# The S5 scan's output products for two state tiles at a time

## The chip, the cores and the metric

The kernel runs on one NeuronCore of a Trainium2 chip. A core has TensorE (matrix products, results in PSUM), VectorE, ScalarE, GpSimd and SyncE, which work side by side, each through its own queue in order, and DMA engines that move data between HBM and the on-chip memory SBUF. The metric is the time of one execution in microseconds on the device. The profiles show each instruction of one execution; the granted TensorE clock is given as a share of full speed.

## The reference

Two layers of an encoder for 256 tokens of width 1024, in float32. Layer 0 normalizes, projects, and splits its columns between an RWKV-7 recurrence (8 heads of 64) and an S5 diagonal state space model; both are concatenated and projected, then come cross-attention to a memory of 256 tokens and a dense SwiGLU. Layer 1 has differential attention, the same cross-attention, and eight SwiGLU experts, two for each token. What matters here is the S5 part: 32 groups of 16 channels, 64 complex states in a group.

```python
_, states = lax.associative_scan(combine, (jnp.broadcast_to(lam_bar, bu.shape), bu), axis=1)
c_mat = lax.complex(c_re.astype(F32), c_im.astype(F32))
y = jnp.real(jnp.einsum('gip,btgp->btgi', c_mat, states))
y = y + d_skip.astype(F32).reshape(S5_GROUPS, S5_GROUP) * ug
y = jax.nn.gelu(y.reshape(b, t, S5_WIDTH))
return y * jax.nn.sigmoid(y @ w_glu.astype(F32) + b_glu.astype(F32))
```

## The kernel before

The program is written in a tile framework. The code issues instructions on named engines; a planner then puts them in an order for each engine, by their priority (mostly the order in which the code issues them) and by a simulated timeline of when each input is ready, and it hands out buffer slots and adds the waits. A pool gives each tag a fixed number of slots; a tile that finds no slot waits until an older tile of its tag is released by its last reader.

The work runs in stages. From about 130 to 350 us three things are mixed, interleaved by `pipeline` (lines 1017 to 1044): the RWKV block matrices and states (`block_matrices`, `block_states`, `block_output`), the S5 scan as a side chain (`s5_scan`), and as filler the key and value projections of both memory attentions (`memory_kv`: cast `fwh` on ScalarE at L450, remainder `fwl` on VectorE at L453, products `pf` at L190 to L192), then the S5 gate (`s5_gate`) and the first half of the output projection. Then come the attention, the dense SwiGLU, layer 1 and the experts, all of which read weights from HBM.

The S5 scan handles the 2048 states in 16 state tiles of 128 rows. Tile j belongs to channel block m = j // 4 and to quarter q = j % 4 of it. For each tile:

- `inputs(j)`: two products of 32 rows into PSUM (`pbu`), VectorE multiplies them with a table into `xc` (L561) and `zz` (L562), GpSimd adds and subtracts (L563, L564);
- `scan(j)`: two scans over 256 tokens on VectorE (L569), `zz` from `xc`; the rotation back: `xc` on VectorE (L571), `zz` on VectorE or GpSimd by turns (L574), and two additions on GpSimd into `xc` (L575, L576), which are the last readers of `zz`;
- `outputs(j)`: two products, `cpad` by the real and by the imaginary half of `xc`, summed into rows 32q to 32q+31 of the PSUM tile `py`, so into a 32-column strip of TensorE's array. Each is shown as two matmul records, since the operands are full float32.

The loop runs `outputs(j - 2)`, `inputs(j)` and `scan(j - 1)` in step j. When the four tiles of a block are in `py`, `gelu(m)` reads it: VectorE L591, ScalarE L593 (the first write of the temporary `t1`), VectorE L594, ScalarE L595, VectorE L596. After steps 5 and 9 the tables of blocks 2 and 3 are made (`s5_table`). `xc`, `zz` and `t1` come from the pool `s5w` with two slots for each tag; `s5_gate` uses `t1` too (L956).

Of the kernel before, what the change touches and what calls it, by code (L numbers as in the profile page):

```python
# [8 lines left out]
F32 = mybir.dt.float32  # L9
# [8 lines left out]
T = 256  # L18
# [53 lines left out]
S5N = 0  # L72
# [51 lines left out]
def kernel(ctx: ExitStack, tc: tile.TileContext, a: dict, out: bass.AP, dbg=None):  # L124
# [10 lines left out]
    def scoped(cx, name, bufs, **kw):  # L135
        return cx.enter_context(tc.tile_pool(name=name, bufs=bufs, reuse_waits="tile", **kw))
# [15 lines left out]
    def col(name, i=0):  # L152
        lo, hi = COLS[name]
        return cols[:, lo + i:lo + i + 1]
# [33 lines left out]
    def mm3(out, lt, r, start, stop, **kw):  # L188

        nc.tensor.matmul(out, lhsT=lt[0], rhs=r[0], start=start, stop=False, **kw)  # L190
        nc.tensor.matmul(out, lhsT=lt[0], rhs=r[1], start=False, stop=False, **kw)  # L191
        nc.tensor.matmul(out, lhsT=lt[1], rhs=r[0], start=False, stop=stop, **kw)  # L192

    def mm(out, lt, r, start=True, stop=True, **kw):
        nc.tensor.matmul(out, lhsT=lt, rhs=r, start=start, stop=stop, **kw)  # L195
# [35 lines left out]
    cx = ExitStack()  # L231
    s5t = scoped(cx, "s5t", 2)
    s5w = scoped(cx, "s5w", 2)
    s5 = scoped(cx, "s5", 1)
    hk = scoped(cx, "hk", 1)
    rk = scoped(cx, "rk", 1)
# [84 lines left out]
    cpad = s5.tile([128, 2, 16, 32], F32, name="cpad")  # L321
# [79 lines left out]
    def s5_table(m):  # L401

        iota = C("iota")
        tbl = s5t.tile([128, 4, 2, T], F32, name="tbl", tag="tbl")
        for q in range(4):
            jc = lambda v: v[:, 4 * m + q:4 * m + q + 1]
            c, s = tbl[:, q, 0], tbl[:, q, 1]
            if TA[m] == "a":
                nc.scalar.activation(s, iota, AF.Copy, bias=MAGIC, scale=jc(fr))
            else:  # L410
                nc.vector.tensor_scalar(s, iota, jc(fr), MAGIC, op0=ALU.mult, op1=ALU.add)
            nc.scalar.activation(c, iota, AF.Copy, scale=jc(fh))
            gstt(c, s, MAGIC, c, op0=ALU.subtract, op1=ALU.subtract)
            gstt(s, iota, jc(fl), c, op0=ALU.mult, op1=ALU.subtract)
        c, s = tbl[:, :, 0], tbl[:, :, 1]
        gts(s, s, 0.5, -0.5, op0=ALU.min, op1=ALU.max)
        nc.scalar.activation(c, s, AF.Abs)
        nc.scalar.activation(c, c, AF.Sin, scale=-6.283185, bias=halfpi)
        nc.scalar.activation(s, s, AF.Sin, scale=6.283185)
        tables.append(tbl)  # L420
# [125 lines left out]
    def s5_scan():  # L546


        xs, zs, pys = {}, {}, {}
        bc2 = lambda v: v[:, None, :].to_broadcast([128, 2, T])  # L550

        def inputs(j):
            m, q = j // 4, j % 4
            rows = slice(32 * q, 32 * q + 32)
            sc = tables[m][:, q]
            pbu = ps_tr.tile([128, 2, T], F32, name="pbu", tag="tr")
            for ri in range(2):
                mm(pbu[:, ri], sbw[rows, ri, m], uT[rows, m])
            xc = xs[j] = s5w.tile([128, 2, T], F32, name="xc", tag="xc")
            z = zs[j] = s5w.tile([128, 2, T], F32, name="zz", tag="zz")  # L560
            nc.vector.tensor_tensor(xc, pbu, bc2(sc[:, 0]), op=ALU.mult)  # L561
            nc.vector.tensor_tensor(z, pbu, bc2(sc[:, 1]), op=ALU.mult)  # L562
            gtt(xc[:, 0], xc[:, 0], z[:, 1], op=ALU.add)  # L563
            gtt(xc[:, 1], xc[:, 1], z[:, 0], op=ALU.subtract)  # L564

        def scan(j):
            xc, z, sc = xs[j], zs[j], tables[j // 4][:, j % 4]
            for ri in range(2):
                nc.vector.tensor_tensor_scan(z[:, ri], rho[:, j:j + 1].to_broadcast([128, T]), xc[:, ri], 0.0,  # L569
                                             op0=ALU.mult, op1=ALU.add)  # L570
            nc.vector.tensor_tensor(xc, z, bc2(sc[:, 0]), op=ALU.mult)  # L571
            e_ = nc.gpsimd if SG[j] == "g" else nc.vector
            if not S5N:
                e_.tensor_tensor(z, z, bc2(sc[:, 1]), op=ALU.mult)  # L574
                gtt(xc[:, 0], xc[:, 0], z[:, 1], op=ALU.subtract)  # L575
                gtt(xc[:, 1], xc[:, 1], z[:, 0], op=ALU.add)  # L576
                return
            e_.tensor_tensor(z[:, 0], z[:, 0], sc[:, 1], op=ALU.mult)
            e_.scalar_tensor_tensor(z[:, 1], z[:, 1], -1.0, sc[:, 1], op0=ALU.mult, op1=ALU.mult)

        def outputs(j):
            m, q = j // 4, j % 4
            if q == 0:
                pys[m] = ps_po.tile([128, T], F32, name="py", tag="po")
            terms = ((0, xs[j][:, 0]), (1, xs[j][:, 1]), (1, zs[j][:, 0]), (0, zs[j][:, 1]))[:4 if S5N else 2]
            for i, (c, x) in enumerate(terms):
                mm(pys[m][32 * q:32 * q + 32], cpad[:, c, j], x, i == 0, i == len(terms) - 1)

        def gelu(m):

            nc.vector.scalar_tensor_tensor(yb[:, m], uT[:, m], col("s5_d", m), pys[m], op0=ALU.mult, op1=ALU.add)  # L591
            t1 = s5w.tile([128, T], F32, name="t1", tag="t1")
            nc.scalar.activation(t1, yb[:, m], AF.Square, scale=math.sqrt(0.044715))  # L593
            nc.vector.scalar_tensor_tensor(t1, t1, 1.0, yb[:, m], op0=ALU.add, op1=ALU.mult)  # L594
            nc.scalar.activation(t1, t1, AF.Tanh, scale=GELU_C)  # L595
            nc.vector.scalar_tensor_tensor(yb[:, m], t1, 1.0, yb[:, m], op0=ALU.add, op1=ALU.mult)  # L596

        for j in range(18):
            if j > 1:
                outputs(j - 2)  # L600
            if j < 16:
                inputs(j)
            if 0 < j < 17:
                scan(j - 1)
            yield 1.3, S5_LAT
            if j > 4 and j % 4 == 1:
                gelu((j - 2) // 4)
            if j in (5, 9):
                s5_table(2 + j // 8)
# [81 lines left out]
    for br, dst in ((0, lw), (1, av)):  # L691
        s = slice(br * 64, br * 64 + 64)
        for m2 in range(2):
            p = ps_mm.tile([128, 2, T], F32, name="pm", tag="mm")
            for j in range(2):
                m = 2 * m2 + j
                mm(p[:, j], wlr[s, m * 128:(m + 1) * 128], zr[s, 0])
            for j in range(2):
                m = 2 * m2 + j
# [244 lines left out]
    def s5_gate():  # L944
        gh, gl = ymix_h[:, 4:8], ymix_l[:, 4:8]
        nc.scalar.activation(gh, yb, AF.Copy, scale=0.5)
        nc.vector.scalar_tensor_tensor(gl, yb, 0.5, gh, op0=ALU.mult, op1=ALU.subtract)
        p = [ps_tr.tile([128, 2, T], F32, name="pm", tag="tr") for _ in range(2)]
        for k, wh, wl in chunks(a["w_glu"], 4):
            for m in range(4):  # L950
                ms = slice(m * 128, m * 128 + 128)
                mm3(p[m // 2][:, m % 2], (wh[:, ms], wl[:, ms]), (gh[:, k], gl[:, k]),
                    k == 0 and m % 2 == 0, k == 3, skip_group_check=True)
            yield 1.3
        for m in range(4):
            t1 = s5w.tile([128, T], F32, name="t1", tag="t1")  # L956
            nc.scalar.activation(t1, p[m // 2][:, m % 2], AF.Tanh, scale=0.5, bias=hcol[:, 8 + m:9 + m])
            nc.vector.scalar_tensor_tensor(yb[:, m], t1, 1.0, yb[:, m], op0=ALU.add, op1=ALU.mult)
        nc.vector.tensor_scalar(yb, yb, 0.25, None, op0=ALU.mult)
        if "yb" in dbg:  # L960
            for m in range(4):
                nc.sync.dma_start(dbg["yb"].rearrange("t (m c) -> m c t", c=128)[m], yb[:, m])
        nc.scalar.activation(ymix_h[:, 4:8], yb, AF.Copy)
        nc.vector.tensor_tensor(ymix_l[:, 4:8], yb, ymix_h[:, 4:8], op=ALU.subtract)
# [26 lines left out]
    def filler():  # L991
        yield from memory_steps
        for _ in s5:
            pass
        yield from s5_gate()
        yield from hy_first()

    s5 = s5_scan()

    def chain():  # L1000
# [1207 lines left out]
```

## Time and profile before

| | |
|---|---|
| three runs | 1668.07, 1673.05 and 1673.32 us, median 1673.05 |
| the profiled execution | 1672.61 us, its span 1670.8 us |
| TensorE busy | 1619.4 us, 97% of the span, 14882 matmul records |
| VectorE, ScalarE, GpSimd busy | 639.9, 476.1, 198.5 us |
| mean granted TensorE clock | 0.976 |
| output products `py` | 64 records, from 132.0 to 266.4 us |

Busy time is the time in which at least one instruction of an engine ran. Matmul records overlap in TensorE's pipeline, so a busy TensorE is not one at its peak; how long a matmul really holds the engine is read from the start of one to the start of the next. The chain of waits follows the work that ended last back from the end: at each step to what released it.

### The profile page before, as it was taken

The page shows a single profiled execution, that of the slowest core. Times are in us where ns is not written, and L with a number is a line of the kernel's source. Part 1 is how long each engine was busy: PE and PEld are TensorE (multiplying, and loading weights), DVE is VectorE, ACT ScalarE, POOL GpSimd, SP SyncE. Part 2 cuts the span into 40 slices and gives each one's busy share as a digit, 9 for nine tenths or more (in the row PEclk, how much of TensorE's full clock was granted, in tenths as well). Part 3 has the DMA queues.
Part 4 walks back from the last instruction along what each step waited for, and adds up shares of the span by engine and source line. Part 5 has one row for each costly group of instructions (what it writes and reads, how often), then busy time and mean ns, then how long its engine had stood idle before and what let it go on. Part 6 is the DMA issues. An engine that isn't in the chain of part 4 may idle for free.

```text
span 1670.8 us, 34308 instructions
## 1 busy us (share of the span) xinstructions
PE 1619.4 (97%) x14882; PEld 982.9 (59%) x14882; DVE 639.9 (38%) x1065; ACT 476.1 (28%) x852; POOL 198.5 (12%) x230
## 2 busy tenths in 40 slices
PE   6999999999999999999999999999999999999997
PEld 5877657899999988998334333343333433333432
DVE  7778987676555567764100011100101001010011
ACT  6466434555544456653101000010000100010000
POOL 6334473111000031110000000000000000000000
PEclk9999979999999999998999999999999999999999
DMA  6423323664555543646699889999999999999995
GB/s 227 152 89 127 109 71 115 222 255 152 186 193 180 195 156 116 239 150 239 252 387 383 333 356 407 415 418 419 419 418 418 419 419 419 418 419 387 372 419 218
DMA packets 74462, 471.48 MB, mean 282 GB/s; under 512 B 8600, under 2 KB 10008, under 8 KB 22464
## 3 DMA queue, kind: packets, MB, share of 16 engines
q1 hardware_dynamic: 73024, 465.02, 71.5%
q0 software_dynamic: 1280, 4.20, 0.7%
q8 instruction: 118, 1.93, 0.5%
q14 instruction: 40, 0.33, 0.1%
HBM read 463.94 MB, written 5.24 MB: 281 GB/s over the span
## 4 chain that ended last, share of the span: by engine, by line
PE 86%; DVE 8%; ACT 2%; POOL 2%; issue 2%; DMA 0%; SPq 0%; DVEq 0%; POOLq 0%; ACTq 0%
PE pgu L195 31%; PE pd L195 16%; PE pm L190 5%; PE pm L192 5%; PE pm L191 5%; PE pgu L190 2%; PE pgu L192 2%; PE pgu L191 2%; PE pm L195 2%; PE pgt L195 1%; PE pf L190 1%; PE pf L191 1%; PE pf L192 1%; PE po L195 1%; DVE zz L569 1%
## 5 line engine op out<-in xcount | busy, mean ns | idle before, releaser
L195 PE MATMUL pgu<-raw,gx 128*32 128x512 f32 (+1 forms) x5376 | 515.8, 542 | 0.0
L195 PEld LDWEIGHTS pgu<-raw,gx 128*32 128x32 f32 x5376 | 171.9, 110 | 319.8 <-issue 287.2
L195 PE MATMUL pd<-raw,th 128*32 128x512 f32 x2352 | 266.4, 607 | 0.4 <-DVE th L1896 0.4
L184 DVE TENSOR_TENSOR wl<-raw,wh 128x1024 fp32r<-128x1024 f32 (+1 forms) x159 | 195.0, 1238 | 103.2 <-ACT wh L178 102.8
L178 ACT ACTIVATE wh<-raw 128x1024 fp32r<-128x1024 f32 (+1 forms) x160 | 165.5, 1047 | 146.8 <-PE pgu L191 67.7
L1882 DVE SCALAR_TENSOR_TENSOR actA<-pgu,gs,actA 128x512 f32<-128x512 f32 (+1 forms) x32 | 21.9, 684 | 468.0 <-PE pgu L195 282.7
L195 PEld LDWEIGHTS pd<-raw,th 128*32 128x32 f32 x2352 | 75.5, 112 | 175.2 <-issue 171.7
L190 PE MATMUL pm<-xh,wh 128*128 128x256 f32 (+1 forms) x552 | 161.6, 296 | 14.4 <-ACT wh L178 12.4
L192 PE MATMUL pm<-xh,wl 128*128 128x256 f32 (+1 forms) x552 | 158.0, 290 | 4.9 <-DVE wl L184 4.9
L191 PE MATMUL pm<-xl,wh 128*128 128x256 f32 (+1 forms) x552 | 159.0, 289 | 2.2 <-DVE xl L1096 2.2
L1878 ACT ACTIVATE actA<-pgu,gs 128x512 f32<-128x512 f32 (+1 forms) x32 | 20.3, 634 | 448.5 <-PE pgu L195 433.5
L190 PEld LDWEIGHTS pm<-xh,wh 128*128 128x128 f32 (+1 forms) x552 | 107.6, 196 | 17.5 <-ACT wh L178 12.9
L192 PEld LDWEIGHTS pm<-xh,wl 128*128 128x128 f32 (+1 forms) x552 | 106.7, 195 | 7.1 <-DVE wl L184 6.4
L191 PEld LDWEIGHTS pm<-xl,wh 128*128 128x128 f32 (+1 forms) x552 | 107.8, 195 | 3.7 <-DVE xl L1096 2.6
L1896 DVE COPY th<-ptA 128x384 f32<-128x384 f32 (+3 forms) x32 | 14.9, 464 | 245.0 <-PE ptA L1895 245.0
L191 PE MATMUL pgu<-xl,wh 128*128 128x256 f32 x352 | 98.6, 280 | 0.0
L190 PE MATMUL pgu<-xh,wh 128*128 128x256 f32 x352 | 98.5, 280 | 0.0
L192 PE MATMUL pgu<-xh,wl 128*128 128x256 f32 x352 | 98.5, 280 | 0.0
L192 PEld LDWEIGHTS pgu<-xh,wl 128*128 128x128 f32 x352 | 66.2, 188 | 0.0
L191 PEld LDWEIGHTS pgu<-xl,wh 128*128 128x128 f32 x352 | 66.2, 188 | 0.0
L190 PEld LDWEIGHTS pgu<-xh,wh 128*128 128x128 f32 x352 | 66.1, 188 | 0.0
L453 DVE SCALAR_TENSOR_TENSOR fwl<-fraw,cols,fwh 128x512 fp32r<-128x512 f32 x64 | 56.9, 896 | 11.4 <-ACT fwh L450 11.3
(477 smaller groups left out, 2138.9 us busy)
## 6 DMA issues: line engine op xcount, KB each, us to landing
raw<-mg SPq DMA_DIRECT2D x112, 1024.0 KB, 15.5
raw<-mu SPq DMA_DIRECT2D x112, 1024.0 KB, 15.3
raw<-md SPq DMA_DIRECT2D x112, 1024.0 KB, 14.9
raw<-wgu SPq DMA_DIRECT2D x22, 1024.0 KB, 4.9
fraw<-wkv SPq DMA_DIRECT2D x32, 512.0 KB, 4.1
raw<-wqkv SPq DMA_DIRECT2D x12, 1024.0 KB, 4.9
raw<-wdn SPq DMA_DIRECT2D x11, 1024.0 KB, 4.9
raw<-hy SPq DMA_DIRECT2D x16, 512.0 KB, 3.8
```

Of the source, the lines that this page charges most:

```text
L178: W["act"].append(nc.scalar.activation(wh, rv, AF.Copy).ins)
L184: W["dve"].append(e_.tensor_tensor(wl[:, c_], rv[:, c_], wh[:, c_], op=ALU.subtract).ins)
L190: nc.tensor.matmul(out, lhsT=lt[0], rhs=r[0], start=start, stop=False, **kw)
L191: nc.tensor.matmul(out, lhsT=lt[0], rhs=r[1], start=False, stop=False, **kw)
L192: nc.tensor.matmul(out, lhsT=lt[1], rhs=r[0], start=False, stop=stop, **kw)
L195: nc.tensor.matmul(out, lhsT=lt, rhs=r, start=start, stop=stop, **kw)
L453: e_.scalar_tensor_tensor(wl, rv, g, wh, op0=ALU.mult, op1=ALU.subtract)
L569: nc.vector.tensor_tensor_scan(z[:, ri], rho[:, j:j + 1].to_broadcast([128, T]), xc[:, ri], 0.0, op0=ALU.mult, op1=ALU.add)
L1878: nc.scalar.activation(actA, p[0], AF.Silu, scale=gs[:, 0, 1:2])
L1882: nc.vector.scalar_tensor_tensor(actA, p[1], gs[:, 0, 1:2], actA, op0=ALU.mult, op1=ALU.mult)
L1896: nc.vector.tensor_copy(th[:, 0], ptA[:, :, 0:c])
```

## The change

The output products are issued for two tiles at once, in the odd steps of the loop: first the real product of both, then the imaginary product of both, which write different 32-row strips of `py`. `xc` moves to a pool of its own with three slots, since a tile now waits for its neighbour. The temporary `t1` of `gelu` and of `s5_gate` gives up its two slots and takes a slot of the tag `zz` instead. Scan, inputs, tables and gate stay tile by tile as they were; a branch for four terms, switched off before, goes.

```diff
     s5w = scoped(cx, "s5w", 2)
+    s5x = scoped(cx, "s5x", 3)
...
-            xc = xs[j] = s5w.tile([128, 2, T], F32, name="xc", tag="xc")
+            xc = xs[j] = s5x.tile([128, 2, T], F32, name="xc", tag="xc")
...
-        def outputs(j):
-            m, q = j // 4, j % 4
-            if q == 0:
+        def outputs(*js):
+            m = js[0] // 4
+            if js[0] % 4 == 0:
                 pys[m] = ps_po.tile([128, T], F32, name="py", tag="po")
-            terms = ((0, xs[j][:, 0]), (1, xs[j][:, 1]), (1, zs[j][:, 0]), (0, zs[j][:, 1]))[:4 if S5N else 2]
-            for i, (c, x) in enumerate(terms):
-                mm(pys[m][32 * q:32 * q + 32], cpad[:, c, j], x, i == 0, i == len(terms) - 1)
+            for c in range(2):
+                for j in js:
+                    q = j % 4
+                    mm(pys[m][32 * q:32 * q + 32], cpad[:, c, j], xs[j][:, c], c == 0, c == 1)
...
-            t1 = s5w.tile([128, T], F32, name="t1", tag="t1")
+            t1 = s5w.tile([128, 2, T], F32, name="t1", tag="zz")[:, 0]
...
         for j in range(18):
-            if j > 1:
-                outputs(j - 2)
+            if j > 1 and j % 2:
+                outputs(j - 3, j - 2)
...
-            t1 = s5w.tile([128, T], F32, name="t1", tag="t1")
+            t1 = s5w.tile([128, 2, T], F32, name="t1", tag="zz")[:, 0]
```

## Rows read from the trace of the kernel before

**Rows 1.** The page's busy times: us (share of the span) and instructions.

```profile
PE 1619.4 (97%) x14882; PEld 982.9 (59%) x14882; DVE 639.9 (38%) x1065; ACT 476.1 (28%) x852; POOL 198.5 (12%) x230
```

**Rows 2.** Busy time by stretch: stretch, its length, each engine's busy us, clock.

```profile
150.00:200.00 50.00, 48.73 (x865) 32.14 (x866) 46.06 (x78) 21.98 (x34) 22.39 (x25) 1.00 0.38 118
...
224.00:242.00 18.00, 17.11 (x293) 10.43 (x293) 16.26 (x27) 6.83 (x17) 13.92 (x18) 0.53 0.08 29
...
257.00:300.00 43.00, 42.84 (x285) 33.76 (x286) 28.20 (x53) 19.57 (x39) 12.10 (x15) 0.96 0.41 138
```

**Rows 3.** The chain that ended last, 130 to 330 us, by line.

```profile
by line: PE pm L195 9.6%; PE pf L190 8.3%; PE pf L191 8.1%; DVE zz L569 8.0%; PE pf L192 7.7%; issue 7.3%; DVE fwl L453 6.3%; PE py L195 3.6%; DVE zz L562 3.4%; PE po L195 3.4%; DVE xc L571 3.1%; DVE xc L561 2.8%; POOL xc L564 2.2%; POOL xc
```

**Rows 4.** TensorE's timeline around output products: start, us to the last end, records.

```profile
132.00 1.06 PE L195 MATMUL py<-xc,cpad 128*32 128x256 f32 x8
133.00 0.44 PE L764 MATMUL pt<-cst,v 128*128 128x128 f32 x2
...
175.95 1.05 PE L195 MATMUL py<-xc,cpad 128*32 128x256 f32 x4
176.93 0.48 PE L195 MATMUL pbu<-uT,sbw 32*128 32x256 f32 x1
...
231.90 1.06 PE L195 MATMUL py<-xc,cpad 128*32 128x256 f32 x2
232.89 0.33 PE L195 MATMUL pm<-qq,vt 32*32 32x32 f32 x8
...
266.19 0.62 PE L195 MATMUL py<-xc,cpad 128*32 128x256 f32 x2
266.74 0.50 PE L192 MATMUL pf<-fwh,mtl 128*128 128x512 f32 x1
```

**Rows 5.** Groups of TensorE's instructions, 130 to 270 us: the output products.

```profile
L195 PE MATMUL py<-xc,cpad 128*32 128x256 f32 x64 | 19.0, 425 | 3.5 <-POOL xc L575 3.0 <-POOL xc L576 0.5
```

**Rows 6.** GpSimd's timeline: last additions of tiles 4, 8, 9, 10, 12, 13.

```profile
165.18 0.90 POOL L576 TENSOR_TENSOR xc<-xc,zz 128x256 f32<-128x256 f32 x1
...
209.50 1.11 POOL L576 TENSOR_TENSOR xc<-xc,zz 128x256 f32<-128x256 f32 x1
...
215.32 1.19 POOL L576 TENSOR_TENSOR xc<-xc,zz 128x256 f32<-128x256 f32 x1
...
224.80 1.10 POOL L576 TENSOR_TENSOR xc<-xc,zz 128x256 f32<-128x256 f32 x1
...
239.20 1.18 POOL L576 TENSOR_TENSOR xc<-xc,zz 128x256 f32<-128x256 f32 x1
...
245.89 1.17 POOL L576 TENSOR_TENSOR xc<-xc,zz 128x256 f32<-128x256 f32 x1
```

**Rows 7.** ScalarE's timeline: the second gelu's first step and what follows it.

```profile
200.62 0.42 ACT L593 ACTIVATE t<-uT 128x256 f32<-128x256 f32 x1 [5.49 <-DVE uT L591]
200.94 1.45 ACT L450 ACTIVATE fwh<-fraw,cols 128x512 fp32r<-128x512 f32 x2
```

**Rows 8.** VectorE's timeline: input products of tiles 6, 10, 11, 14; second gelu's end.

```profile
178.77 0.68 DVE L562 TENSOR_TENSOR zz<-pbu,tbl 128x512 f32<-128x512 f32 x1
...
207.65 0.41 DVE L596 SCALAR_TENSOR_TENSOR uT<-t,uT 128x256 f32<-128x256 f32 x1
...
213.31 0.68 DVE L561 TENSOR_TENSOR xc<-pbu,tbl 128x512 f32<-128x512 f32 x1
213.91 0.68 DVE L562 TENSOR_TENSOR zz<-pbu,tbl 128x512 f32<-128x512 f32 x1
...
221.01 0.68 DVE L561 TENSOR_TENSOR xc<-pbu,tbl 128x512 f32<-128x512 f32 x1
...
244.86 0.68 DVE L562 TENSOR_TENSOR zz<-pbu,tbl 128x512 f32<-128x512 f32 x1
```

**Rows 9.** Busy time by stretch, columns as in rows 2: two slow stretches.

```profile
207.20:210.60 3.40, 3.40 (x34) 1.87 (x32) 3.40 (x7) 2.89 (x4) 1.79 (x2) 0.50 0.54 159
224.30:241.30 17.00, 16.41 (x291) 9.99 (x291) 15.26 (x24) 6.26 (x16) 13.62 (x17) 0.50 0.05 17
```

## The prediction

> **What bounds the kernel now.** I read the page first. TensorE is busy 97% of a span of 1670.8 us [rows 1], but that is a mean over stages, and matmul records overlap. The edit touches one stage only, the one in which the S5 scan, the RWKV blocks and the memory projections run mixed together, from about 130 to 350 us. After it the kernel streams weights, and nothing there is edited. A gain or a loss in this stage passes on to the end one for one, since no later work can start before the stage ends.
>
> So I cut the stage with the table of stretches [rows 2]. Two parts differ. From 150 to 242 us the clock falls and VectorE is about as full as TensorE (46.06 of 50 us, then 16.26 of 18), GpSimd is three quarters full at the end (13.92 of 18), and TensorE runs from 224 to 242 us at a granted clock of 0.53. There the latency of the scan counts: matmul, two VectorE products, two GpSimd additions, scan, product, rotation, additions, and back to TensorE. From 257 us TensorE is full (42.84 of 43) and VectorE has a third of its time free (28.20 busy). The chain of waits [rows 3] says the same: no line holds even a tenth of it, and the edited product (`py`) stands in it with 3.6% of 200 us, 7.2 us. The scan's `zz` and `xc` lines on VectorE hold 17.3%.
>
> **Part 1, the products side by side.** One state tile has two output products, each a pair of matmul records with 128 rows, 32 columns and 256 moving columns. The timeline of TensorE [rows 4] has all the cases that matter. Two products of one tile back to back, from the first record to the next other matmul: 176.93 - 175.95 = 0.98 us. One product alone between other matmuls: 266.74 - 266.19 = 0.55. One alone at the half clock: 232.89 - 231.90 = 0.99. And, at the start, tiles 0 and 1 together, eight records: 133.00 - 132.00 = 1.00 us. So two tiles, in different 32-column strips, cost what one costs. The side by side order is worth a factor of two here, and the trace shows it without the edit, because the instruction planner happened to put tiles 0 and 1 together.
>
> The 32 products stand in 23 groups of the timeline, first at 132.00, last at 266.19 [rows 4]: one of 1.00, five of 0.98, eleven of 0.55, one of 0.56 (two tiles together again), four at the half clock of 0.99, one of 0.88 across a change of clock. Sum 17.4 us. In the new form there are eight groups: seven at 1.00 and, if the tiles 10 and 11 stay in the slow stretch, one at about 1.8: 8.8 us. **TensorE is relieved of at most 8.6 us.** It reaches the end only where TensorE is what ends last. Lower end: nothing, if VectorE and GpSimd set the pace. Upper end: 8.6. I take the share that the chain of waits gives: 7.2 us x 8.6/17.4 = **-3.6 us**.
>
> **Part 2, waiting at the head of TensorE.** The products waited 3.5 us for GpSimd's two additions [rows 5]. What stands behind them in TensorE's queue are the next tile's input products and the memory projections. In a pair the earlier tile has no wait left, but the later one has the same two. Between 0 and half of it, -1.7; I take 0, since a wait for the second tile may now hold back both tiles' products.
>
> **Part 3, the later issue of the even tile.** Its products move one loop step later. Nothing but `gelu` and the slot of `xc` waits for them. `gelu(m)` needs the odd last tile of its four anyway. `xc` gets three slots instead of two, so tile j+3 instead of j+2 waits for the pair. At the end of the loop, four products follow the last addition instead of two; side by side they take 1.00 us against 2 x 0.55 [rows 4]. Cost 0; were the pair split there, +1.1.
>
> **Part 4, the temporary of `gelu` in the ring of `zz`.** This is the part that can cost. `t1` had two slots of its own; now it takes one of the two `zz` slots. A `zz` slot is free only when GpSimd's last addition (L576) has read it. For the second gelu: `t1` is written at 200.62 [rows 7], but tile 8's slot is free at 209.50 + 1.11 = 210.6 and tile 9's at 215.32 + 1.19 = 216.5 [rows 6]. So `t1` waits 10 us, and tile 10, whose `zz` is written at 213.91 [rows 8] into tile 8's slot, must wait for tile 9's, 216.5: 2.6 us later. Third gelu: slots free at 240.4 and 247.1, tile 14's write at 244.86: 2.2 us. First gelu: `t1` could start at 166.1 and take what the second took, 200.62 to 208.06, 7.4 us: done by 173.5, before tile 6's write at 178.77: nothing. Last gelu, behind the last scan: nothing. Later `gelu` results cost nothing by themselves, since their next reader is the gate, which needs the last gelu anyway. What queues behind the waiting write on ScalarE is the memory projections' cast (`fwh`, at 200.94 [rows 7]); were the planner to leave the write at its old place, the casts and with them VectorE's `fwl` and TensorE's projections would stand still for up to 10 us. It knows the slots, so I put the write behind the casts.
>
> So the scan's chain slips by 4.8 us in all. Cover: VectorE and TensorE have memory projections to do meanwhile, and TensorE is the bound from 257 us. If the cover holds, 0; if the scan is the path throughout, +4.8. I take half, **+2.4**, as the stretch is mixed.
>
> **Part 5, the whole order.** The planner orders the stage anew, with everything in it. No row prices that. The largest single thing that an order can lose or win is the stretch of 17 us at clock 0.50 [rows 9], in which a product takes 0.99 instead of 0.55: about 8.5 us of TensorE's time. Zero in the sum, this in the range. SBUF is the same: three `xc` slots of 2 KB a partition against two, and two `t1` slots of 1 KB less. No DMA is added.
>
> **Sum.** -3.6 + 0 + 0 + 2.4 = -1.2 us. The profiled execution took 1672.61, 0.44 under the median; 1.8 of it lies outside the span. **1671.4 us.**
>
> **Rivals.**
>
> *All of it counts.* TensorE's in-order queue holds the memory projections' buffers too, so any time freed is used, and the slot costs nothing: 1672.6 - 8.6 = **1664.0**. For it: the full stretches from 257 us. Against: only the last two tiles' products, four of 32, lie there. Chance 0.24.
>
> *The shared slot decides (slower).* The place is tile 10 and tile 14. With one slot gone, a tile can't be in flight beside the one before: tile 10 needs from 213.31 (its first product, 0.60 before its `zz` write) to the end of its last addition, some 12.6 us, where the next started 7.7 us behind it. Losing that overlap, 4.9 us, at both places: +9.8, less the 3.6 of part 1: **1678.8**. It decides once the scan slips by more than 3.6 + 5.0 us, and if nothing covers it. For it: the lines of `zz` and `xc` in the chain. Against: TensorE's full stretches behind it. Chance 0.20.
>
> *It doesn't pair.* The planner issues a product when its input is ready; in the second half a tile's products stand right behind its own additions and 6 to 7 us ahead of the next tile's, so the even tile may go alone as before. Then only part 4 is left: **1675.0**. Chance 0.14.
>
> *The clock falls oftener.* The granted clock is 0.50, the lower level of 1.2 GHz, for 17 us from 224 us, where VectorE and GpSimd carry the scan, and for 3.4 us at 207 us [rows 9]. With less work TensorE waits oftener. Two more stretches like the short one, each losing half of 3.4 us: 1671.4 + 3.4 = **1674.8**. Against: freed time is filled with projections. Chance 0.06. The Trainium skill ("TensorE: Matmul & The Clock Gate", Part 1) says that the throttled clock is the default and that activity releases it; this speaks against giving TensorE less to do, and the trace agrees in that its long slow stretch lies where the scan sets the pace.
>
> **How the numbers follow.** 0.3%, about what a measurement of this kernel can tell from no change, is 5.0 us. My own case has 0.36, with a range of 1667 to 1676. Faster: the first rival, but for a part of it that lands short, 0.22, and 0.06 of my own: 0.28. Slower: 0.18 of the second, 0.03 of the others: 0.21. Same: 0.51. The range goes to what parts 1, 2 and 5 could win together (-8.6 - 1.7 and some of the clock, 1661) and to the slow rival with some of the clock against it, 1682.
>
> **What would show it.** Part 1: eight groups of eight `py` records of 1.0 us, their sum under 10 us. If the groups still have two or four, it didn't pair. Part 4: `t1`'s first write (L593 before) behind an end of GpSimd's last addition, tile 10's and 14's `zz` writes later against their neighbours. Part 5: length and place of the half-clock stretches. I am wrong if the stage ends over 5 us earlier or later, with the later stages unchanged: earlier if the products were all on the path, later if the scan is.

## The result and the profile after

The changed kernel takes 1681.39 us (median of 7 runs, 1673.73 to 1683.69), the kernel before 1673.05 (7 runs, 1668.07 to 1676.79): a ratio of 1.0054, 95% interval 1.0038 to 1.007. It is slower by 0.5%. The forecast was 1671.4 us, with no change the likeliest; the range, 1661 to 1682, holds the time, but the kernel moved the other way, and by more than its interval. A second comparison of the same two kernels gave 1.0050 (1.0032 to 1.0068). The ratios here and below are taken over all runs of a comparison, and differ a little from the quotient of two medians. The profile below is of a run of 1683.4 us, span 1681.6, granted clock 0.971 (before: span 1670.8, clock 0.976). In the changed file the lines of the scan stand one or three further down: L561 is L562, L562 is L563, L576 is L577.

The page's busy times, in answer to [rows 1]:

```profile
PE 1619.5 (96%) x14882; PEld 988.7 (59%) x14882; DVE 639.1 (38%) x1065; ACT 475.9 (28%) x852; POOL 198.5 (12%) x230
```

The same work, the same busy time on every engine, 10.8 us more span. So the loss is idle time and clock, and the sums of an engine can't show it. By stretch, in answer to [rows 2]:

```profile
150.00:200.00 50.00, 42.13 (x837) 30.35 (x836) 43.95 (x79) 26.15 (x38) 21.73 (x22) 0.97 0.38 117
...
224.00:242.00 18.00, 15.37 (x289) 9.73 (x289) 17.17 (x27) 6.55 (x21) 12.36 (x16) 0.70 0.15 46
...
257.00:300.00 43.00, 42.73 (x287) 33.66 (x286) 27.40 (x51) 18.63 (x38) 11.24 (x14) 0.94 0.35 118
```

From 150 to 200 us TensorE is now busy for 42.13 us where it was for 48.73: the relief is there, and something else as well, since it is more than the output products hold. TensorE's timeline around them, in answer to [rows 4] (start, us to the last end, records):

```profile
190.31 0.62 PE L195 MATMUL py<-xc,cpad 128*32 128x256 f32 x2
190.86 0.50 PE L190 MATMUL pf<-fwh,mth 128*128 128x512 f32 x1
...
213.84 1.06 PE L195 MATMUL py<-xc,cpad 128*32 128x256 f32 x8
214.82 0.48 PE L195 MATMUL pbu<-uT,sbw 32*128 32x256 f32 x1
...
225.71 1.77 PE L195 MATMUL py<-xc,cpad 128*32 128x256 f32 x8
227.41 0.48 PE L195 MATMUL pbu<-uT,sbw 32*128 32x256 f32 x1
```

Two tiles together take 214.82 - 213.84 = 0.98 us, what one took before, and 227.41 - 225.71 = 1.70 us in the slow stretch. Some products still stand alone (190.31). The group of all of them, in answer to [rows 5]:

```profile
L195 PE MATMUL py<-xc,cpad 128*32 128x256 f32 x64 | 12.2, 411 | 0.1
```

19.0 us have become 12.2, and the 3.5 us that TensorE waited for them 0.1. By the prediction's own measure, from the first record of a group to the next other matmul, 17.4 us in 23 groups have become 11.4 us in 13, and only three of these are full pairs of eight records. Part 1's mechanism is there, at 6.0 us of a possible 8.6. What TensorE waits for instead, from 130 to 345 us, first before and then after (us in total, times, longest):

```profile
PE py L195 <- POOL xc L575: 3.0, 3, 1.5
PE pf L191 <- DVE fwl L453: 2.0, 2, 1.4
PE pbu L195 <- DVE zz L562: 1.2, 2, 0.9
PE pf L190 <- ACT kx L492: 0.6, 1, 0.6
PE py L195 <- POOL xc L576: 0.5, 1, 0.5
```

```profile
PE pf L191 <- DVE fwl L454: 5.0, 3, 3.0
PE pm L195 <- DVE arb L798: 3.2, 1, 3.2
PE ptf L509 <- ACT kx L505: 2.6, 1, 2.6
PE pm L195 <- DVE qq L826: 1.7, 1, 1.7
PE pf L190 <- ACT wh L178: 1.6, 1, 1.6
PE pm L195 <- DVE w L831: 0.8, 1, 0.8
PE pf L192 <- DVE wl L184: 0.5, 1, 0.5
...
```

7.3 us of waiting have become 16.0 (with two of 0.3 that are not shown). The waits are for VectorE's and ScalarE's part of RWKV and of projections; of the scan there is left one of the two of 0.3, for `zz`.

**The first loss lies ahead of the stage.** Matching the products of both traces, the changed kernel is 0.1 us ahead until 50 us and 4.1 us behind from 60 to 130 us, where nothing is paired yet. VectorE and TensorE there, before:

```profile
50.77 1.22 DVE L184 TENSOR_TENSOR wl<-raw,wh 128x1024 fp32r<-128x1024 f32 x1
51.90 0.68 DVE L617 TENSOR_TENSOR zm<-pm,rsB 128x512 f32<-128x512 f32 x1
...
52.73 0.36 PE L190 MATMUL pm<-xh,wh 128*128 128x256 f32 x1 [1.94 <-DVE zm L617]
```

and after, with GpSimd's line of the wait:

```profile
47.02 0.68 DVE L562 TENSOR_TENSOR xc<-pbu,tbl 128x512 f32<-128x512 f32 x1
...
51.25 1.21 DVE L184 TENSOR_TENSOR wl<-raw,wh 128x1024 fp32r<-128x1024 f32 x1
...
53.01 0.72 POOL L577 TENSOR_TENSOR xc<-xc,zz 128x256 f32<-128x256 f32 x1
...
53.76 0.69 DVE L563 TENSOR_TENSOR zz<-pbu,tbl 128x512 f32<-128x512 f32 x1 [1.29 <-POOL xc L577]
54.37 0.68 DVE L620 TENSOR_TENSOR zm<-pm,rsB 128x512 f32<-128x512 f32 x1
...
54.60 2.04 PE L195 MATMUL pbu<-uT,sbw 32*128 32x256 f32 x4 [3.32 <-DVE zz L563]
56.57 0.58 PE L190 MATMUL pm<-xh,wh 128*128 128x256 f32 x1
```

At 47.02 stands the first input product of tile 2. Before, that tile could not start until tile 0's output products gave back an `xc` slot at 132 us [rows 4]. The third slot lets the planner issue it 86 us earlier than before, when it stood at 133.1. Its `zz` has no third slot: it waits for tile 0's last addition (53.01 + 0.72 = 53.73) at the head of VectorE's queue, and the read-out of a projection (`zm`, 51.90 before, 54.37 now) queues behind it. TensorE then does the next tile's input products first, and takes up the projections at 56.57 instead of 52.73. The two stretches of 47 to 60 us (columns as in [rows 2]), before and after:

```profile
47.00:60.00 13.00, 10.56 (x73) 9.77 (x71) 11.70 (x20) 5.41 (x7) 7.61 (x8) 0.87 0.41 130
```

```profile
47.00:60.00 13.00, 8.55 (x44) 7.05 (x43) 11.71 (x19) 2.79 (x4) 8.72 (x9) 0.75 0.40 126
```

44 matmul records instead of 73, and the clock at 0.75 instead of 0.87.

**The rest of the loss lies behind the dense SwiGLU.** The first and last of its input products of line 192, before and after (durations in ns, then first and last start):

```profile
L192 PE MATMUL pgu<-xh,wl x352: 277/280/287, 405.2 to 581.3; 128*128 128x256 f32 x176
```

```profile
L192 PE MATMUL pgu<-xh,wl x352: 277/280/287, 410.7 to 586.8; 128*128 128x256 f32 x176
```

The dense SwiGLU starts 5.5 us late, so the mixed stage adds 1.4 us to the 4.1. From the last of these products to the end it is 1670.8 - 581.3 = 1089.5 us before and 1681.6 - 586.8 = 1094.8 after: 5.3 us more in code that the change doesn't touch, and in which TensorE has the same instructions in the same order. The experiments take these two halves one after the other.

### The profile page after: what moved, and what is told of

Same layout as the page of the kernel before. It is cut to its first block, busy times and chain, and to the rows that moved or that the text cites. A ratio compares the mean times of both kernels' runs of the same rounds, so it can differ in the third digit from the quotient of the medians.

```text
span 1681.6 us, 34318 instructions
## 1 busy us (share of the span) xinstructions
PE 1619.5 (96%) x14882; PEld 988.7 (59%) x14882; DVE 639.1 (38%) x1065; ACT 475.9 (28%) x852; POOL 198.5 (12%) x230
## 4 chain that ended last, share of the span: by engine, by line
PE 87%; DVE 7%; ACT 2%; issue 2%; POOL 1%; DMA 0%; SPq 0%; DVEq 0%; POOLq 0%; ACTq 0%
PE pgu L195 30%; PE pd L195 16%; PE pm L190 6%; PE pm L192 5%; PE pm L191 5%; PE pgu L190 2%; PE pgu L191 2%; PE pgu L192 2%; PE pf L190 2%; PE pm L195 2%; PE pf L191 2%; PE pf L192 2%; PE pgt L195 1%; PE po L195 1%; PE psc L195 1%
## 5 line engine op out<-in xcount | busy, mean ns | idle before, releaser
L190 PE MATMUL pm<-xh,wh 128*128 128x256 f32 (+1 forms) x552 | 161.9, 296 | 12.2 <-ACT wh L178 12.2
L192 PE MATMUL pm<-xh,wl 128*128 128x256 f32 (+1 forms) x552 | 158.0, 290 | 4.2 <-DVE wl L184 4.2
L190 PEld LDWEIGHTS pm<-xh,wh 128*128 128x128 f32 (+1 forms) x552 | 107.6, 196 | 16.0 <-ACT wh L178 12.8
L192 PEld LDWEIGHTS pm<-xh,wl 128*128 128x128 f32 (+1 forms) x552 | 106.6, 195 | 6.6 <-DVE wl L184 5.7
L192 PE MATMUL pgu<-xh,wl 128*128 128x256 f32 x352 | 98.6, 280 | 0.0
L190 PE MATMUL pgu<-xh,wh 128*128 128x256 f32 x352 | 98.6, 281 | 0.0
L192 PEld LDWEIGHTS pgu<-xh,wl 128*128 128x128 f32 x352 | 66.3, 188 | 0.0
L190 PEld LDWEIGHTS pgu<-xh,wh 128*128 128x128 f32 x352 | 66.2, 188 | 0.0
## 6 DMA issues: line engine op xcount, KB each, us to landing
raw<-mg SPq DMA_DIRECT2D x112, 1024.0 KB, 15.9
```

## The experiments

Four theories. **A**: the third `xc` slot draws tile 2 forward and blocks VectorE at 52 us, +4 us. **B**: the `zz` slot shared with `t1` costs, as part 4 of the prediction had it. **C**: the third slot costs throughout the stage, since tiles run ahead of their `zz` slots. **D**: it is only another order; the pairs are worth nothing, and what a new order loses is chance. All ratios are to the kernel before, run on the same chip, with 95% intervals.

**The shared slot, alone and taken out (B).** The kernel before with only `t1` in the ring of `zz`, and the changed kernel with `t1` in a part of `sbw` that is no longer read:

```diff
 # e3_t1_zz, on the kernel before
-            t1 = s5w.tile([128, T], F32, name="t1", tag="t1")
+            t1 = s5w.tile([128, 2, T], F32, name="t1", tag="zz")[:, 0]
 # e1_t1_free, on the changed kernel
-            t1 = s5w.tile([128, 2, T], F32, name="t1", tag="zz")[:, 0]
+            t1, y2 = sbw[:, :, m], yb[:, m].rearrange("p (a b) -> p a b", a=2)
```

> The kernel before, tile by tile and with two xc slots, with the temporary in the zz ring alone. Theory A: tile 2 starts at 133 us as before, no step near 55 us, 1671 to 1676 us. Theory B: gelu and tiles 10 and 14 wait for each other, 1677 to 1682 us.

> The changed kernel, but gelu's temporary lies in a part of the input matrices that is no longer read, so it takes no zz slot. Theory A (the third xc slot lets tile 2's input products go 80 us earlier, and its zz write then stands at the head of VectorE's queue): the step of about 4 us near 55 us stays, 1677 to 1682 us. Theory B (the shared zz slot costs): the loss goes, 1671 to 1675 us.

Alone: 1669.27 us, 0.9987 (0.9977 to 0.9996). Taken out: 1681.57, 1.0058 (1.004 to 1.0076). B falls in both directions: in the whole time the slot costs nothing alone and gives nothing back. The first of these, which came in under what either theory had, is also the one kernel of the study that beats both, by 0.13%, at the highest mean clock of all, 0.9815 against 0.9766 before.

**The third slot alone (A, C).** The kernel before, tile by tile, with `xc` in three slots; `t1` lies in `sbw` as above, to make the room.

```diff
+    s5x = scoped(cx, "s5x", 3)
...
-            xc = xs[j] = s5w.tile([128, 2, T], F32, name="xc", tag="xc")
+            xc = xs[j] = s5x.tile([128, 2, T], F32, name="xc", tag="xc")
```

> The kernel before, tile by tile, with the third xc slot alone (the temporary in the input matrices, where it waits for nothing). Theory A: tile 2's zz write waits in VectorE's queue near 50 us, the work behind it is about 4 us late, 1676 to 1679 us. Theory B: as before, 1671 to 1675 us.

1683.33 us, 1.0065 (1.0045 to 1.0084): no product is paired, and the whole loss is there, more than A had put on tile 2 alone. Its VectorE shows the same block:

```profile
47.58 0.68 DVE L562 TENSOR_TENSOR xc<-pbu,tbl 128x512 f32<-128x512 f32 x1
...
54.32 0.69 DVE L563 TENSOR_TENSOR zz<-pbu,tbl 128x512 f32<-128x512 f32 x1 [1.29 <-POOL xc L577]
54.93 0.68 DVE L618 TENSOR_TENSOR zm<-pm,rsB 128x512 f32<-128x512 f32 x1
```

Tile 2 is not the only one: the `zz` of tiles 2, 5, 7 and 8 is written 6.7, 12.3, 5.9 and 2.1 us behind their `xc`, where the kernel before has 0.5 to 0.7 us for every tile. This run also shows what the pairs are worth, since it and e1 have the same slots and the same place for `t1` and differ in the pairs alone: 1.0065 without them and 1.0058 with them, intervals that overlap almost wholly.

**Holding tile 2 back (A against C).** The changed kernel, with tile 2's two products on VectorE issued only after the last read-out of the third projection.

```diff
-            nc.vector.tensor_tensor(xc, pbu, bc2(sc[:, 0]), op=ALU.mult)
-            nc.vector.tensor_tensor(z, pbu, bc2(sc[:, 1]), op=ALU.mult)
+            with tc.issue_after(W["zlast"]) if j == 2 else ExitStack():
+                nc.vector.tensor_tensor(xc, pbu, bc2(sc[:, 0]), op=ALU.mult)
+                nc.vector.tensor_tensor(z, pbu, bc2(sc[:, 1]), op=ALU.mult)
...
-            nc.vector.tensor_tensor(z[:, 2 * m2:2 * m2 + 2, 1:], p[m2], rsb(2), op=ALU.mult)
+            W["zlast"] = nc.vector.tensor_tensor(z[:, 2 * m2:2 * m2 + 2, 1:], p[m2], rsb(2), op=ALU.mult).ins
```

> The changed kernel in full, but the two VectorE input products of tile 2 are ordered behind the last product of the third RWKV projection (where they stood before). Theory A: the step of 4 us near 55 us is gone, 1675 to 1678 us, and any loss that is left lies after 130 us. Theory B: no gain, 1679 to 1683 us.

1681.26 us, 1.0061 (1.0042 to 1.008). The step at 55 us is gone (-0.3 us to 130 us), and yet nothing is won: between 130 and 350 us the kernel loses 15.9 us. Two stretches there, columns as in [rows 2]:

```profile
158.70:179.20 20.50, 20.50 (x197) 13.25 (x192) 14.60 (x24) 8.54 (x11) 8.38 (x9) 0.50 0.23 75
240.60:261.10 20.50, 15.12 (x203) 9.01 (x205) 18.68 (x26) 5.31 (x16) 17.65 (x21) 0.50 0.15 52
```

41 us at half clock, against 17 and 3.4 in [rows 9]. A alone is not the answer: the time that the hold saves at 55 us is lost again in the stage. A third slot for `zz` too, which would let an early tile through, was not tried.

**No tile runs ahead at all (C against D).** A rule that holds tiles 2 and 3 behind the projection and every later tile behind the rotation of the one before it, and issues a scan ahead of the next inputs. It is put into the changed kernel (e5), the third slot alone (e6) and, as control, the kernel before (e8).

```diff
-        xs, zs, pys = {}, {}, {}
+        xs, zs, pys, held = {}, {}, {}, {2: W["zlast"], 3: W["zlast"]}
...
+            with tc.issue_after(held[j]) if j in held else ExitStack():
...
-            nc.vector.tensor_tensor(xc, z, bc2(sc[:, 0]), op=ALU.mult)
+            held.setdefault(j + 1 if j else 99, nc.vector.tensor_tensor(xc, z, bc2(sc[:, 0]), op=ALU.mult).ins)
...
-            if j < 16:
+            if j < 4:
                 inputs(j)
             if 0 < j < 17:
                 scan(j - 1)
+            if 3 < j < 16:
+                inputs(j)
```

> The changed kernel in full, with the input products of every tile from 2 on kept from running ahead on VectorE: tiles 2 and 3 behind the third RWKV projection's last product, tile j behind the rotation of tile j-1. Theory C (the third xc slot costs because tiles run ahead): most of the loss goes, 1667 to 1675 us, and what the pairs are worth shows against the next run. Theory D (the order of the stage is merely another one, and the pairs are worth nothing): 1677 to 1684 us.

> The kernel before, tile by tile, with the third xc slot (its own run was 1683 us) and the same rule against running ahead. Theory C: 1670 to 1676 us. Theory D: 1677 to 1684 us.

> Control: the kernel before with two xc slots and the rule against running ahead, which its order nearly keeps already. Both theories: 1670 to 1675 us; if it is over 1677, the rule itself costs and the two runs with it tell nothing.

Changed kernel 1.0029 (1.0016 to 1.0042), third slot alone 1.0017 (1.0007 to 1.0028), before 1.0025 (1.0014 to 1.0037). The rule by itself costs a quarter of a per cent, so that the control (1675.95 us) and e5 (1675.83) lie just over the ranges that C had for them; under it the three are alike within 0.12%, and the intervals overlap. So where nothing runs ahead, the third slot costs nothing (C holds: 1.0017 against 1.0065 without the rule, intervals well apart). The place of `t1`, which e2 changed as well, is the same in e6, and so it isn't the cause either. The pairs bring nothing (D's half of it holds too), though the group of output products falls from 18.1 us in the control to 13.6 in e5. VectorE under the rule, changed kernel: `zm` is back behind `wl`, at 52.94:

```profile
51.80 1.21 DVE L184 TENSOR_TENSOR wl<-raw,wh 128x1024 fp32r<-128x1024 f32 x1
52.94 0.68 DVE L623 TENSOR_TENSOR zm<-pm,rsB 128x512 f32<-128x512 f32 x1
```

**What TensorE's time is worth here.** The kernel before, with nothing paired: half of its output products left out (e9; each tile issues only the product of its real half), and each tile's products issued twice (e10).

```diff
 # e9_half
-            for i, (c, x) in enumerate(terms):
-                mm(pys[m][32 * q:32 * q + 32], cpad[:, c, j], x, i == 0, i == len(terms) - 1)
+            for i, (c, x) in enumerate(terms[:1]):
+                mm(pys[m][32 * q:32 * q + 32], cpad[:, c, j], x, True, True)
 # e10_double
+            for i, (c, x) in 2 * list(enumerate(terms)):
```

> The kernel before with 16 of the recurrence's 32 output products left out (every tile issues only the product of its real half, so the S5 output lacks its imaginary part); nothing is paired and no buffer changes. Their TensorE time falls from 17.4 us to about 8.7 us, a little more than the pairs take away (17.4 to about 11 us). If the relief of the pairs is worth nothing because TensorE waits for VectorE or GpSimd in those places anyway: within 0.3% of before, 1667 to 1677 us, and the mixed stage ends within 2 us of where it did. If TensorE's time is on the path and only something else in the change eats it: 4 to 8 us faster (1664 to 1668 us), with the first dense SwiGLU product 4 to 8 us earlier than 404.9 us.

> The kernel before with each tile's pair of output products issued twice (the second time over the first, so the numbers are the same): 17.4 us more of TensorE. If this stage's TensorE time is on the path: 10 to 17 us slower. If there is cover for it: under 5 us slower. It is the counterpart of the run with half the products; the same price per us in both directions would say that TensorE's time there is on the path, and a loss here without a gain there that the cover is just used up.

Both lose. Twice the products: 1690.39 us, 1.0118 (1.0096 to 1.014); their group rises by 13.0 us, from 19.0 to 32.0, and the dense SwiGLU starts 17.3 us later, more than the forecast's 10 to 17 in the whole time (19.6). Half of them: 1679.94 us, 1.0053 (1.0035 to 1.0071), which no theory had: their group falls by 8.4 us, to 10.6, and the dense SwiGLU starts 7.9 us later, at 412.8. Its slow stretches:

```profile
204.80:215.00 10.20, 9.82 (x146) 6.55 (x145) 10.20 (x18) 6.33 (x8) 4.77 (x6) 0.50 0.32 104
228.70:242.40 13.70, 9.72 (x165) 5.72 (x164) 12.96 (x21) 4.11 (x10) 9.98 (x14) 0.50 0.05 20
262.80:279.90 17.10, 16.16 (x86) 13.78 (x87) 6.99 (x18) 6.35 (x16) 2.29 (x5) 0.50 0.20 79
```

With a fourth, 3.4 us from 334.5 us on, that is 44.4 us at half clock, against 23.8 in the stage before: 3.4 and 17.0 of [rows 9], and

```profile
258.40:261.80 3.40, 3.40 (x10) 2.46 (x8) 3.23 (x4) 0.72 (x1) 2.31 (x2) 0.50 0.22 43
```

The longest stretch lies where TensorE is full (16.16 of 17.10): there half clock is lost time, up to half of 17.1 us. It isn't the one profile alone: over all runs of this comparison the mean granted clock is 0.9714 with half of the products, 0.9773 with twice and 0.9777 before. An estimate from these: (0.9777 - 0.9714) / 0.5 x 1670 = 21 us more at half clock, worth up to 10.5 us, so the clock is enough for the whole loss of 9. So taking work off TensorE, with no slot changed, can cost as much as the change did. The order is planned anew in this run too, so it stays open whether less work or another order brought the clock down.

**The order within a pair, and the changed kernel again.** The changed kernel with the products in tile order, both of one tile and then both of the other, run in two comparisons, in the second beside the changed kernel itself.

```diff
-            for c in range(2):
-                for j in js:
-                    q = j % 4
+            for j in js:
+                q = j % 4
+                for c in range(2):
```

> The changed kernel with the same slots and steps, but in the odd steps the four products stand tile by tile again, not side by side. If the pairs are worth TensorE time on the path, it is 2 to 7 us slower than the changed kernel, 1683 to 1688 us. If not, the same, 1679 to 1683 us.

> The changed kernel itself, unchanged, beside the unpaired one on the same chip: 1.004 to 1.007 of before, about 1681 us. If it and the unpaired one differ by under 0.15%, the pairs are worth nothing and the difference seen between separate comparisons was one of the comparison.

> The changed kernel with the two tiles' products issued tile after tile instead of side by side, a second time, on the same chip as the changed kernel. If the pairs themselves cost nothing and bring nothing: the same as the changed kernel within 0.15%, so 1.004 to 1.007 of before. If the side-by-side order itself costs something (a changed clock, another plan): 1.001 to 1.003 as the first time, 4 to 6 us under the changed kernel.

Tile order 1674.95 us, 1.0020 (1.0008 to 1.0031), under both of the first forecast's cases, and then 1.0025 (1.001 to 1.0041); the changed kernel 1.0050 (1.0032 to 1.0068). The runs are called unpaired, but the pairs are still there. In the second, the group of output products is 11.3 us, and TensorE shows

```profile
137.22 1.08 PE L195 MATMUL py<-xc,cpad 128*32 128x256 f32 x12
138.22 0.44 PE L767 MATMUL pt<-cst,v 128*128 128x128 f32 x2
```

three tiles, issued one after the other (all of one tile, then all of the next), in 1.00 us. It is enough that they stand next to each other in the queue. So this run doesn't undo the pairs, and its median still differs from the changed kernel's by 6 us, though the intervals of the second comparison overlap. In the profiles of the second comparison, 1680.5 and 1672.4 us of span, 0.6 us of the difference is there by the dense SwiGLU's end (586.1 and 585.5); the rest lies behind it, where the two issue the same instructions in the same order but for two late groups of the experts' products. Two slow stretches of the changed kernel there, and tile order at the first place, 0.6 us earlier, and with its own slow stretch near the second:

```profile
616.10:622.90 6.80, 6.80 (x19) 5.49 (x19) 0.17 (x1) 0.00 (x0) 3.72 (x3) 0.50 0.01 2
790.20:807.20 17.00, 13.44 (x65) 9.14 (x63) 11.40 (x58) 2.23 (x7) 2.35 (x4) 0.50 0.45 160
```

```profile
615.50:622.30 6.80, 6.80 (x33) 5.57 (x33) 1.25 (x4) 1.66 (x2) 4.78 (x4) 1.00 0.01 2
788.60:798.80 10.20, 6.64 (x32) 4.99 (x35) 7.94 (x45) 1.30 (x4) 2.16 (x3) 0.50 0.47 177
```

At 616 us TensorE is full in both and gets 19 matmul records through in one and 33 in the other. The waits ahead of it are the same (2.2 us in two, for VectorE's `xl`).

**Does the time of arrival decide that clock?** 48 products more in the third block of the dense SwiGLU, 5.7 us, in the kernel before (e13), the changed one (e15) and tile order (e16), and 90, 10.7 us, in the kernel before (e14). They repeat products over themselves.

```diff
                 for m in range(2):
+                    for _ in range(8 if i == 2 and k == 0 else 0):
+                        mm3(p[m][:, 0], (wh[:, m * 128:m * 128 + 128], wl[:, m * 128:m * 128 + 128]),
+                            (xt[0][:, k], xt[1][:, k]), True, False, skip_group_check=True)
```

> The kernel before with 48 more products in the dense SwiGLU's third block (its first products issued again over themselves, same numbers): 48 times 0.119 us = 5.7 us, so that everything behind begins 5.7 us later, about as late as in the changed kernel. If the tail's clock hangs on when it begins: the stretch from the last dense SwiGLU input product to the end is no longer 1089.6 us but moves by 3 us or more, towards 1094, and the time is about 1681 us. If the tail is the kernel's own and a delay is only a delay: 1676.5 us, tail 1089 to 1090.

> The same with 90 more products, 10.7 us. Delay only: 1681.5 us, tail 1089 to 1090. If the tail hangs on when it begins, it moves by 2 us or more in either direction from 1089.6.

> The changed kernel with the same 48 products, 5.7 us later. Delay only: 1686.4 us, tail still 1094 to 1095, with a half-clock stretch of 6.8 us about 15 us behind the dense SwiGLU's end. If the tail hangs on when it begins: the tail falls or rises by 3 us or more and that stretch is gone or another.

> The changed kernel with the two tiles' products in tile order, 5.7 us later by the same 48 products. Delay only: 1680.3 us, tail 1087. If the tail hangs on when it begins: the tail moves by 3 us or more, and its advantage over the changed kernel (6 us in the comparison without the delay) changes with it.

The rows of the table come from four comparisons; each ratio is to the kernel before in its own. The median of the first row is that of the comparison with the delays.

| | median us | ratio (95%) | first dense product, L190 | last, L192 | span | last to end |
|---|---|---|---|---|---|---|
| before | 1673.11 | | 404.9 | 581.3 | 1670.8 | 1089.5 |
| before, 5.7 later | 1680.14 | 1.0050 (1.0032 to 1.0067) | 403.3 | 585.3 | 1676.3 | 1091.0 |
| before, 10.7 later | 1682.84 | 1.0069 (1.0047 to 1.009) | 405.7 | 592.6 | 1679.4 | 1086.8 |
| changed | 1681.39 | 1.0054 (1.0038 to 1.007) | 410.4 | 586.8 | 1681.6 | 1094.8 |
| changed, again | 1680.65 | 1.0050 (1.0032 to 1.0068) | 409.8 | 586.1 | 1680.5 | 1094.4 |
| changed, 5.7 later | 1683.92 | 1.0070 (1.0048 to 1.0092) | 411.1 | 593.0 | 1682.1 | 1089.1 |
| tile order | 1674.95 | 1.0020 (1.0008 to 1.0031) | 411.5 | 587.9 | 1674.9 | 1087.0 |
| tile order, again | 1674.6 | 1.0025 (1.001 to 1.0041) | 409.1 | 585.5 | 1672.4 | 1086.9 |
| tile order, 5.7 later | 1686.04 | 1.0074 (1.0047 to 1.0101) | 413.7 | 595.7 | 1687.5 | 1091.8 |

Beginning later, the tail of the changed kernel is 5.7 us shorter, that of tile order 4.9 longer, that of before moves by +1.5 and -2.7. The 6 us that parted the changed kernel from tile order are gone in the medians too (1683.92 against 1686.04, with overlapping intervals). So the tail is not the change's own: it takes between 1086.8 and 1094.8 us, and the longer ones have more time at half clock (40.3 us before, 51.1 in the changed kernel, 33.8 in tile order, again). That the arrival decides it is not shown, though: the executions of one and the same kernel differ by as much, the changed kernel's seven from a span of 1671.9 us at a clock of 0.977 to 1681.9 at 0.970, and each tail here is that of one execution. What decides it stays open.

The other column is steadier. Three profiles of before start the dense SwiGLU at 403.3, 404.9 and 405.7 us, three of the changed kernel at 409.8, 410.4 and 411.1. The means differ by 5.8 us. **That is what the change costs up to there**; the measured 8 to 10 us have, by subtraction, some 2 to 4 of the tail on top. By the same column, with one profile each, the third slot alone (e2) starts it at 415.4 us, the changed kernel without the shared slot (e1) at 415.1, and the shared slot alone (e3) at 403.1; under the rule it is 406.2 (e5), 407.5 (e6) and 405.8 (control). So up to there the third slot costs 10.5 us, the pairs give back 0.3 and the shared slot some 4.7, which the whole times, with the tail in them, don't show.

The clock has a large part in the loss. Over all runs of the second comparison the mean granted clock is 0.9734 in the changed kernel and 0.9777 before. An estimate from these: (0.9777 - 0.9734) / 0.5 x 1670 = 14 us more at half clock, and where TensorE is the bound up to 7 us of the 8 to 10. How the third slot, or the order that came with it, brings the clock down is not shown.

## Why the prediction was wrong

By its own sign, a stage that ends over 5 us later, the prediction is wrong, if by little: 5.5 us in the first profile, 5.8 in the means of three.

- **Part 3 is the step that failed:** "`xc` gets three slots instead of two, so tile j+3 instead of j+2 waits for the pair. [...] Cost 0". I looked at who waits longer and not at who may now start sooner. A planner that sorts by what is ready uses a free slot, and the write after it (`zz`) had no slot to match. Tile 2's `zz` then stood at the head of VectorE's queue, and TensorE was 4.1 us behind at 60 us. The third slot alone brings the loss (1.0065), and it is free where tiles may not run ahead (1.0017 beside 1.0025 for the control).
- **Part 1 was right about the array and wrong about the path.** Relief 6.0 us for 8.6, since some products still go alone. The share by the chain of waits, -3.6, didn't come: e1 and e2, which differ in the pairs alone, start the dense SwiGLU at 415.1 and 415.4 us; the waits grew from 7.3 to 16.0 us, and with 8.4 us of products simply left out the stage ended later. A line's share of a chain says what stood on the path, not what the stage would do without it.
- **Part 2** had 0 in the sum, and nothing was won. Its reason doesn't hold: it feared that both tiles' products would wait for the second, but the wait went from 3.5 to 0.1 us, more than the half that it allowed. The time saved was waited for something else.
- **Part 4 had the wait right and the price, +2.4, wrong.** In e3, where the shared slot is the only change, `t1` of the second gelu and tile 10's `zz` wait as worked out: `t1` starts at 211.49 us (200.62 before), and tile 10's `zz` stands at 216.62, behind tile 9's last addition, 3.0 us behind its `xc`:

```profile
211.49 0.40 ACT L593 ACTIVATE t<-uT 128x256 f32<-128x256 f32 x1
...
215.69 0.72 POOL L576 TENSOR_TENSOR xc<-xc,zz 128x256 f32<-128x256 f32 x1
...
216.62 0.68 DVE L562 TENSOR_TENSOR zz<-pbu,tbl 128x512 f32<-128x512 f32 x1
```

  That run is not slower (0.9987), so the wait is covered. In the changed kernel tile 10's `zz` doesn't wait, and a wait of the kind appears at tile 6, whose `xc` is written at 159.07 and its `zz` at 169.01, behind the last use of the first gelu's `t1`:

```profile
159.07 0.68 DVE L562 TENSOR_TENSOR xc<-pbu,tbl 128x512 f32<-128x512 f32 x1
...
167.73 0.58 DVE L599 SCALAR_TENSOR_TENSOR uT<-t,uT 128x256 f32<-128x256 f32 x1 [0.98 <-ACT t L598]
...
169.01 0.69 DVE L563 TENSOR_TENSOR zz<-pbu,tbl 128x512 f32<-128x512 f32 x1
```

  Before, that `zz` stood at 178.77 [rows 8], so the wait takes only time that was won by running ahead. Without the shared slot (e1) tile 6's `zz` is written at 161.55, and the dense SwiGLU starts 4.7 us later: here the slot holds back a tile that would run ahead. That this is why it helps is not shown.
- **Part 5** had the size: runs in which the planner orders the stage anew lie from -0.13% (e3) to +0.65% (e2), though none of them changes the order alone. The long slow stretch itself was not the loss: 224 to 242 us has a clock of 0.70 for 0.53. Slow stretches at other places took its part: from 130 to 345 us the clock is at half for 29.4 us, against 23.8.
- **The rivals.** "The shared slot decides" came near the time, 1678.8, by a mechanism that isn't there. "All of it counts" and "it doesn't pair" are out. "The clock falls oftener", at 0.06, was worth more: the mean granted clock fell from 0.978 to 0.973, and leaving out products was followed by some 20 us more of half clock in the stage. The rule of the Trainium skill named beside it ("TensorE: Matmul & The Clock Gate", Part 1: the throttled clock is the default, and activity releases it) agrees in direction with the trace of the run with half the products, 44.4 us of half clock for 23.8, though that run has another order as well.

## What to carry to other kernels

Under a planner, a wider ring is a change like a narrower one: ask which tile may now start early, and which of its later writes has no slot and will stand at the head of an in-order queue; hold the chain back, which took back most of the loss here and won nothing (e5, e6), or widen the rings of one chain together, which was not tried. Time taken from the busiest engine counts only if nothing else is late next: leave the work out in a trial, before rewriting it. And compare the end of the stage that was edited in several profiles, since the time of the whole holds the clock of everything behind it.

## What the runs showed of the hardware

- Output products in different 32-column strips run side by side also when they are issued one tile after the other: three tiles in 1.00 us, one in 0.98 [rows 4], so 3 x 0.98 / 1.00 = 2.9 times as fast. The Trainium skill ("TensorE: Matmul & The Clock Gate", section "Why this matters for your kernels") gives 2.38 for three tiles of 32 columns, at another width; the trace agrees that they overlap, and here they do so almost fully.
- The same work, in the same order on TensorE, took 1089.5 us in the kernel before and 1094.8 in the changed one, with 40.3 and 51.1 us of it at half clock. One unchanged kernel's executions go from a span of 1671.9 us at a mean clock of 0.977 to 1681.9 at 0.970.
- Leaving out 8.4 us of products made a kernel 0.5% slower, at a mean clock of 0.971 for 0.978.
